# A hybrid attention and MLP step on one core: sixteen-bit transposes by transfer, 33 groups of seven, alternating chunk order in the first part

## The chip, the cores and the metric

The kernel runs on one core of a Trainium2 chip. The metric is the device time of one execution in microseconds. The engines are PE (TensorE: matmuls and transposes), DVE (VectorE), ACT (ScalarE), POOL (GpSimd) and SP (SyncE, which here only issues transfers); sixteen DMA engines carry the transfers that SP, ACT and POOL issue. PEld is the loading of the stationary operand into PE.

## The reference

One layer for 128 context tokens and 128 latent tokens, model width 2048, in float32:

```
sh1, sc1, g1, sh2, sc2, g2 = split(silu(c) @ w_ada + b_ada)
h  = rms_norm(x) * (1 + sc1) + sh1
qa, ka, va, qb, kb, vb, ga, gb = split(h @ w_in)        # 2048 x 8704
oa = windowed attention (qa, ka, va);  ob = neighbourhood attention (qb, kb, vb)
x  = x + g1 * ((sigmoid(ga) * (oa @ w_br_a) + sigmoid(gb) * (ob @ w_br_b)) @ w_out)
h2 = rms_norm(x) * (1 + sc2) + sh2
x  = x + g2 * (relu(h2 @ w_up) ** 2 @ w_down)           # 2048 x 8192 x 2048
```

Both token groups use the same weights, so a weight tile is read once and multiplied with both (the index `s` or `tb`, 0 or 1). The outputs are the two token groups and the keys and values of the context.

## The kernel before

**Products in three parts.** A float32 product is made of three matmuls: each operand is split into a high half (rounded to the matmul's type) and a low half (the rest), and high x high, high x low and low x high are summed in PSUM. For a weight tile `raw` [128, 1024] (two blocks of 128 rows, 512 columns) ACT makes the high half (`copy`, line 86, tile `wH`) and DVE the low half by a subtraction (line 234, tile `wL`). For some steps (`LO_DMA`) the low half is made by ACT and an accumulating transfer of POOL's queue instead (`minus_plus`, line 238). Activations are split in the same way (`split`, line 88).

**Steps.** The program is a list of 456 steps, one for each weight tile of 512 KB, in an order fixed by hand. `run` (line 257) goes through them: it issues the loads of SP up to step i + `LOAD` + `RUN[i]` (4 plus a digit), prepares the halves up to step i + `LOOK[i]` (a digit), emits the step's matmuls (`mm`) and then what the calendar holds for the step (`at(i, fn)`). Every engine works through its own instructions in that order. Tiles of 4 KB per partition come from one ring of 48 buffers (`G`, line 76); a load waits until its buffer is free.

**The parts.** Steps 0 to 71 are the first part: nine units of 512 columns of `w_in` (`first_units`), whose 2048 rows are taken in five chunks (`CHUNKS`, tiles of 128 rows: 2, 2, 2, 4, 6). For each chunk all nine units are run in the same order (`start_steps`, line 370). At the end of a unit's chunk ACT copies the two PSUM accumulators to SBUF (first chunk, `first_evac`) or DVE adds them there (line 393). Meanwhile the modulation is computed (`w_ada` on PE as `ps_ada`, or as dot products on DVE, line 1278, `DOTS1`, `DOTS`, `DOTS2`). Steps 72 to 135 are the gate columns of `w_in` with the attention between them; steps 136 to 167 the branches (`br_unit`, line 805), 168 to 199 `w_out`. Then come the sixteen units of `w_up` (512 columns each), in pairs (`PIECES`), with the `w_down` units of the pair before: the pair p + 1 of `w_up` (16 steps), then the four `w_down` units of pair p (16 steps).

**Groups of seven.** In pairs 1 to 7 of `w_up` a position (two steps) is either plain, 8 products, or one of the positions in `FAST`, where the 2 x 2 block product (two token groups, two blocks of rows, two units) is made of seven products of sums (`up_pair`, line 1058; `prep_y`, line 1115). A product is three matmuls. Such a position needs more sums and halves on DVE and ACT.

**Transposes.** Matmuls contract over partitions, so the merged branches (four tiles) and the sixteen results of `w_up` have to be transposed before they are multiplied on. `tT` (line 792) does this on PE: for each token group four transposes of 128 x 128 into one PSUM bank (`ps_T`, line 797), a copy by ACT (the high half) and a subtraction by DVE (line 800). Its calls stand two steps after a branch unit's end (line 823), in `up_unit` and `up_pair` for the first two `up` tiles, and at `T_PAIR` steps after a pair's end for the others (line 1237).

**Sums of `w_down`.** A unit's accumulators are added to `dsum` by DVE (line 1210) or, for the units in `SUM_DMA`, copied by ACT and added by an accumulating transfer on POOL's queue (line 1214).

**Gates.** The eight gate tiles wait in SBUF until their branch; those in `AWAY` go to memory and come back (`unit_gate`, `gate_back`).

Of the kernel before, what the change touches and what calls it, by code (L numbers as in the profile page):

```python
# [10 lines left out]
F32 = mybir.dt.float32  # L11
F32R = mybir.dt.float32r
BF16 = mybir.dt.bfloat16
AF = mybir.ActivationFunctionType
OP = mybir.AluOpType
AX = mybir.AxisListType

P = 128
# [13 lines left out]
FB_DVE = 6  # L32
FB1 = 14
H_AT = 41
DOTS1 = [6, 8, 15, 20, 28, 30, 31, 38]
CHUNKS = [2, 2, 2, 4, 6]
NFAST = 8
FAST = {1: (0, 1, 5, 6, 7), 2: (0, 3, 4, 6, 7), 3: (0, 2, 4, 5, 7), 4: (0, 2, 3, 5, 7), 5: (0, 1, 2, 4, 5, 7), 6: (0, 2, 4, 6, 7), 7: (0, 1, 2, 4, 5, 7)}
# [7 lines left out]
LOOK = "523112344222344433223333332123333453344534332454455544344533333544324554444555556665556644444333333333332222122213444544555434333333342344333334333323445565533344456656533344434444445455564546555554444443322355444554433333333434334433333333333654654332334455554444555653323314333422222223443233333332223323365455454443222212233432443334434743443332222333423323333333333325434322223333433323333334555543365365433333332222554442122132334343222223332233345544"  # L46
RUN = "454562331000011222223333322222222222222233345555544455434445554445665555555664543433234334444445665543321222222212444444444444442222222232223344444455544544444444443344343334466644455555554543255444343355556866544443566553333323333345552332222222223445332333333333332211122222332233322211233323323332333223333333332343322211333343333322233333444433643333312222334443322333233322222222322333443434455544333120222222232111233456655566567556322325335553333333"
CONST_AT = [60, 65]
XL_DMA = [40]
ADA_AT = [None, 4, 13, 21, 21, 34, 30]  # L50
XS_AT = {1: 13, 2: 18, 3: 29}
POST = {('kvA', 0): [67, 69, 71], ('qA', 0): [70, 73, 75], ('qA', 1): [74, 76, 82], ('kB', 0): [78, 84, 89], ('qB', 0): [82, 84, 93], ('kB', 1): [85, 90, 93], ('qB', 1): [91, 94, 96]}
JOBS = [[78, 79, 81, 83, 94], [82, 83, 87, 90, 94], [88, 89, 91, 93, 98], [93, 93, 95, 98, 102], [96, 97, 100, 105, 112], [102, 103, 107, 112, 120], [105, 107, 111, 118, 120], [112, 114, 117, 120, 122]]
SS_AT = [48, 56, 66, 75, 139, 139]
T_AT = [4, 4]
PREP_IN = [6, 7]
DOTS = [32, 39, 41, 43, 47, 47, 48, 49, 51, 52, 53, 55, 60, 64, 67, 69, 72, 76, 76, 83, 89, 90, 92, 92, 94, 98, 101, 103, 103, 105, 108, 111, 111, 112, 115, 118, 120, 122, 123, 123, 124, 128, 129, 129, 131, 132, 133, 137, 137, 137, 138, 143, 144, 147, 147, 150, 153, 157, 158, 160, 165, 167, 168, 168, 170, 172, 175, 177, 177, 178, 179, 183]
DOTS2 = [232, 233, 235, 237, 240, 242, 262, 265, 269, 270, 272, 289, 297, 299, 302, 306, 307, 326, 327, 332, 334, 335, 358, 361, 364, 365, 368, 370, 393, 394, 397, 401]
STAT_AT = [-1, -1, 10, 12]
# [5 lines left out]
def tile_hybrid_step(ctx: ExitStack, tc: tile.TileContext, a):  # L65
# [16 lines left out]
    def bank(name, pool_=None):  # L82
        return (pool_ or paux).tile([P, 512], F32, name=name, tag="b")
# [278 lines left out]
    nf = len(first_units)  # L362
    units = {}

    def first_evac(u, acc):
        units[u] = G(f"u_{u[0]}{u[1]}").rearrange("p (s n) -> p s n", s=2)
        for tb in range(2):
            copy(units[u][:, tb, :], acc[tb])

    def start_steps(u, k0, nk):  # L370

        box = {}

        def mm(st, kt):
            if kt == 0:
                box["acc"] = [bank("acc", pacc) for _ in range(2)]
            acc = box["acc"]
            wh, wl = st["hl"]
            last = kt + 2 == nk
            for k in range(2):  # L380
                g, kg = divmod(k0 + kt + k, 4)
                for tb in range(2):
                    sh, sl = hH[g][:, kg, tb, :], hL[g][:, kg, tb, :]
                    pe.matmul(acc[tb], sh, wh[:, k, :], start=kt == 0 and k == 0, stop=False)  # L384
                    pe.matmul(acc[tb], sh, wl[:, k, :], start=False, stop=False)  # L385
                    pe.matmul(acc[tb], sl, wh[:, k, :], start=False, stop=last and k == 1)  # L386
            if not last:
                return
            if k0 == 0:
                first_evac(u, acc)  # L390
                return
            for tb in range(2):
                dve.tensor_tensor(units[u][:, tb, :], units[u][:, tb, :], acc[tb], op=OP.add)
# [384 lines left out]

    def sigmoids():
        for u in gates:  # L780
            if u not in direct:
                sigmoid(u)

    sig_at = end_of(("gA", DIRECT[0] - 1)) + 2
# [2 lines left out]


    mH, mL = [None] * 4, [None] * 4
    mt = {}  # L790

    def tT(src, hi, lo):

        for s in range(2):
            ps = bank("ps_T")
            for k in range(4):
                pe.transpose(ps[:, k * P:(k + 1) * P], src[:, s, k * P:(k + 1) * P], ident)  # L797
            psv = ps.rearrange("p (k t) -> p k t", k=4)
            copy(hi[:, :, s, :], psv)
            dve.tensor_tensor(lo[:, :, s, :], psv, hi[:, :, s, :].bitcast(F32), op=OP.subtract)  # L800

    def HL(name):
# [24 lines left out]

    br0 = len(wsteps)
    for n in range(4):
# [131 lines left out]
    split_unit(a["w_out"], 512 * 3, m_stat, evac_out3, ("out", 3), norm2_at(1, 0))  # L961


    aH, aL = {}, {}
    up_r = {}

    def h2_stat(j):
        return lambda kk, tb: (h2H[j][:, kk, tb, :], h2L[j][:, kk, tb, :])

# [15 lines left out]
        sync.dma_start(t, x1d[n])  # L985
        x1[n] = t.rearrange("p (s n) -> p s n", s=2)

    def up_T(n):
        aH[n], aL[n] = HL(f"a{n}")
        tT(up_r.pop(n), aH[n], aL[n])  # L990
# [12 lines left out]

# [54 lines left out]
    def up_pair(p):  # L1058
# [32 lines left out]
        for pos, is_fast in enumerate(kinds):  # L1091
# [50 lines left out]
            def mm_y(st, b=b, j=j, pos=pos, end=end):  # L1142
# [11 lines left out]
                if pos == 0:  # L1154
                    for name, stat, h, l in todo[0:3]:
                        mm(name, stat, h, l, end)
                    if p == 1:
                        up_T(PIECES[0][1])
# [290 lines left out]
```

## Time and profile before

| | |
|---|---|
| Median of three runs | 1346.45 us (1346.03 to 1346.79) |
| The profiled execution | 1346.98 us |
| Its span, first to last instruction | 1344.9 us |
| Granted TensorE clock | 0.997 |
| Bytes moved | 385.44 MB, 287 GB/s |

The profile has a page (busy time of each engine, the span in slices, the DMA queues, the chain of work that ended last, the costliest groups) and views of the same trace: busy time in stretches ("windows"), waits by releaser, the instructions of one tile, the chain in order of time, the timeline. A group's row reads: line, engine, operation, out<-in, form, count, then busy time in us, mean ns of one, and the idle time before it with what ended it. A row of the chain is its start, its length and what it was. A row of windows has each engine's busy time and, in brackets, its count of instructions; PEclk is the granted clock, and the DMA share is the mean busy share of the sixteen DMA engines. Matmuls are pipelined: the duration of one is longer than the distance to the next.

### The profile page before, as it was taken

The numbers are of one execution on the slowest core, as the hardware profiler recorded it, in microseconds if no ns is written. First come the engines' busy times: TensorE is split into PE (matmuls) and PEld (weight loads), VectorE is DVE, ScalarE is ACT, GpSimd is POOL, SyncE is SP. The second block draws the span as 40 slices with busy tenths as digits, with TensorE's granted clock in tenths as the row PEclk, the third lists the DMA queues.
The fourth block names the chain that finished last, engine by engine and source line by source line (L and its number), as shares of the span: only waits on it lengthen the run. The fifth ranks groups of instructions, "written<-read, shape, count | busy, mean of one in ns | idle before, by whom it ended". The sixth has DMA issues, their size and how long they took to land.

```text
span 1344.9 us, 18331 instructions
## 1 busy us (share of the span) xinstructions
PE 1331.6 (99%) x6552; PEld 1081.6 (80%) x6552; DVE 1194.9 (89%) x1568; ACT 738.8 (55%) x966; POOL 66.7 (5%) x76
## 2 busy tenths in 40 slices
PE   8899999999999999999999999999999999999998
PEld 4577788888788878888888888888888888888887
DVE  4689999988898999998789999998999999899675
ACT  5524443566656544345666665565665656556540
POOL 0000001332000000000000000000000000000000
PEclk9899999999999999999999999999999999999999
DMA  9999998977688999798466666888798887769942
GB/s 370 410 409 408 404 366 352 375 215 271 193 282 299 377 397 344 284 332 290 175 232 230 240 219 245 271 264 279 231 317 239 265 285 216 267 191 302 373 151 93
DMA packets 109611, 385.44 MB, mean 287 GB/s; under 512 B 12368, under 2 KB 13584, under 8 KB 109520
## 3 DMA queue, kind: packets, MB, share of 16 engines
q1 hardware_dynamic: 104064, 365.05, 73.5%
q0 software_dynamic: 5312, 19.14, 7.5%
q8 instruction: 51, 0.84, 0.3%
q14 instruction: 40, 0.33, 0.1%
q10 hardware_dynamic: 144, 0.08, 0.0%
HBM read 369.25 MB, written 7.11 MB: 280 GB/s over the span
## 4 chain that ended last, share of the span: by engine, by line
PE 96%; DMA 3%; DVE 1%; issue 0%; ACT 0%; SPq 0%; DVEq 0%
PE acc L284 17%; PE acc L286 17%; PE acc L285 17%; PE Q L1068 6%; PE Q L1070 6%; PE Q L1069 6%; PE acc L384 4%; PE acc L386 4%; PE acc L385 4%; PE ps_ada L301 2%; DMA raw<-in_w_in 2%; PE ps_T L797 1%; PE ps_S L700 1%; DMA araw<-in_w_pair 1%; PE Z L1070 1%; PE Z L1069 1%
## 5 line engine op out<-in xcount | busy, mean ns | idle before, releaser
L234 DVE TENSOR_TENSOR wL<-raw,wH 128x1024 fp32r<-128x1024 f32 x361 | 430.7, 1225 | 79.6 <-ACT wH L86 72.6
L86 ACT ACTIVATE wH<-raw 128x1024 fp32r<-128x1024 f32 (+1 forms) x385 | 385.6, 1047 | 138.6 <-PE acc L285 33.0
L384 PE MATMUL acc<-wH,hH 128*128 128x512 f32 x276 | 109.9, 398 | 0.0
L386 PE MATMUL acc<-wH,hL 128*128 128x512 f32 x276 | 108.4, 393 | 0.7 <-DVE hL L90 0.7
L385 PE MATMUL acc<-wL,hH 128*128 128x512 f32 x276 | 108.5, 393 | 0.0
L284 PE MATMUL acc<-wH,hH 128*128 128x512 f32 x256 | 101.8, 398 | 0.0
L286 PE MATMUL acc<-wH,hL 128*128 128x512 f32 x256 | 99.8, 390 | 0.0
L285 PE MATMUL acc<-wL,hH 128*128 128x512 f32 x256 | 99.7, 389 | 0.0
L1278 DVE CUSTOM_DVE_ANT_0 aT<-aT,cB,cols 128x1024 f32<-128x1024 f32 x56 | 71.5, 1284 | 0.2
L1278 DVE CUSTOM_DVE_ANT_0 junk<-aT,cB,cols 128x1024 bf16<-128x1024 f32 x56 | 71.3, 1279 | 0.0
L86 ACT ACTIVATE tH<-t 128x1024 fp32r<-128x1024 f32 x37 | 39.3, 1062 | 56.9 <-DVE t L1123 42.0
L384 PEld LDWEIGHTS acc<-wH,hH 128*128 128x128 f32 x276 | 52.3, 190 | 14.2 <-issue 3.3
L386 PEld LDWEIGHTS acc<-wH,hL 128*128 128x128 f32 x276 | 52.4, 190 | 12.3 <-DVE hL L90 1.1
L385 PEld LDWEIGHTS acc<-wL,hH 128*128 128x128 f32 x276 | 52.4, 190 | 10.5
L86 ACT ACTIVATE uH<-raw 128x1024 fp32r<-128x1024 f32 x37 | 39.3, 1063 | 36.2 <-DVE raw L1128 35.2
L286 PEld LDWEIGHTS acc<-wH,hL 128*128 128x128 f32 x256 | 48.1, 188 | 10.3
L285 PEld LDWEIGHTS acc<-wL,hH 128*128 128x128 f32 x256 | 48.1, 188 | 9.6 <-issue 0.2
L284 PEld LDWEIGHTS acc<-wH,hH 128*128 128x128 f32 x256 | 48.1, 188 | 9.6 <-issue 0.2
L1123 DVE TENSOR_TENSOR t<-raw 128x1024 f32<-128x1024 f32 x37 | 45.1, 1220 | 5.8 <-PE Z L1069 1.9
L1176 ACT ACTIVATE up<-up 128x1024 f32<-128x1024 f32 x28 | 29.7, 1062 | 33.0 <-DVE up L1170 32.6
L86 ACT ACTIVATE dsum<-acc 128x512 f32<-128x512 f32 x38 | 22.0, 595 | 45.2 <-PE acc L286 42.1
L1133 DVE TENSOR_TENSOR uL<-raw,uH 128x1024 fp32r<-128x1024 f32 x37 | 45.1, 1219 | 0.1
(629 smaller groups left out, 3320.4 us busy)
## 6 DMA issues: line engine op xcount, KB each, us to landing
raw<-in_w_in SPq DMA_DIRECT2D x133, 512.0 KB, 6.7
raw<-in_w_down SPq DMA_DIRECT2D x128, 512.0 KB, 5.9
araw<-in_w_pair SPq DMA_DIRECT2D x80, 512.0 KB, 9.6
raw<-in_w_upF SPq DMA_DIRECT2D x74, 512.0 KB, 5.2
aT<-in_w_gT SPq DMA_DIRECT2D x64, 512.0 KB, 6.6
raw<-in_w_up SPq DMA_DIRECT2D x54, 512.0 KB, 5.1
aT<-in_w_adaT SPq DMA_DIRECT2D x48, 512.0 KB, 7.4
raw<-in_w_out SPq DMA_DIRECT2D x32, 512.0 KB, 9.5
```

The source lines that it names most:

```text
L86: act.activation(out, in_, AF.Copy)
L234: dve.tensor_tensor(st["lo"], st["raw"], st["hi"].bitcast(F32), op=OP.subtract)
L284: pe.matmul(acc[tb], sh, wh[:, k, :], start=f, stop=False)
L285: pe.matmul(acc[tb], sh, wl[:, k, :], start=False, stop=False)
L286: pe.matmul(acc[tb], sl, wh[:, k, :], start=False, stop=l)
L384: pe.matmul(acc[tb], sh, wh[:, k, :], start=kt == 0 and k == 0, stop=False)
L385: pe.matmul(acc[tb], sh, wl[:, k, :], start=False, stop=False)
L386: pe.matmul(acc[tb], sl, wh[:, k, :], start=False, stop=last and k == 1)
L1068: pe.matmul(acc, stat[0], hi, start=f, stop=False)
L1069: pe.matmul(acc, stat[0], lo, start=False, stop=False)
L1070: pe.matmul(acc, stat[1], hi, start=False, stop=l)
L1278: dve.tensor_tensor_reduce(out, box["raw"], cB[s, tag], 1.0, dst if second else baT[:, part, fb:fb + 1], OP.mult, OP.add, dst)
```

## The change

Four things are done together, with the constants of the order set anew.

1. *Transposes by transfer.* For the sixteen `up` tiles and three of the four merged tiles (`M_TE` keeps the last on PE) the calls of `tT` give way to three steps of the calendar. `part`: ACT copies the low and the high 16 bits of each float32 into two planes of a `U16` tile. `flip`: SP issues one transposing transfer of that tile, 16 blocks of 128 x 128, into another tile. `join`: ACT puts the two planes together again into a float32 tile, and `split` makes the two halves (a copy on ACT, a subtraction on DVE). `flip` stands one step (`FLIP`), for the merged tiles two steps, after `part`; `join` stands 3 to 5 steps after `flip` for the tiles of the later pairs, 6 for the merged ones, and 1 and 3 for the first two `up` tiles.
2. *Groups of seven* go from 37 to 33: `FAST[1]` from 5 to 3, `FAST[2]` from 5 to 4, `FAST[5]` from 6 to 5.
3. *First part.* Every second chunk takes the units in reverse, so that the last unit of a chunk is the first of the next; its two accumulators stay in PSUM across the turn.
4. *Placement.* `LO_DMA` goes from 18 to 12 steps, `XL_DMA` from one to none, `SUM_DMA` from 15 to 10 units, `AWAY` from three to six gate tiles, which come back earlier (`GATE_BACK` 3 to 8). `LOOK`, `RUN` and the lists of steps are set anew; their mean over a part changes by less than about one step.

```
 FAST before = {1: (0, 1, 5, 6, 7), 2: (0, 3, 4, 6, 7), 3: (0, 2, 4, 5, 7), 4: (0, 2, 3, 5, 7), 5: (0, 1, 2, 4, 5, 7), 6: (0, 2, 4, 6, 7), 7: (0, 1, 2, 4, 5, 7)}
 FAST after  = {1: (0, 3, 7), 2: (0, 2, 6, 7), 3: (0, 2, 4, 5, 7), 4: (0, 2, 4, 5, 7), 5: (0, 3, 4, 5, 7), 6: (0, 2, 4, 5, 7), 7: (0, 1, 2, 4, 5, 7)}
-SUM_DMA = [5, 6, 9, 10, 11, 12, 13, 15, 16, 19, 20, 21, 23, 25, 27]
+SUM_DMA = [5, 6, 11, 13, 16, 19, 21, 23, 25, 27]
-AWAY = [('gA', 1), ('gB', 0), ('gA', 2)]
+AWAY = [('gA', 1), ('gB', 2), ('gB', 3), ('gA', 0), ('gB', 0), ('gA', 2)]
-GATE_BACK = 3
+GATE_BACK = 8
-LO_DMA = [70, 83, 86, 107, 131, 176, 184, 186, 196, 233, 242, 292, 314, 328, 357, 379, 402, 435]
+LO_DMA = [70, 83, 107, 131, 176, 184, 233, 292, 314, 328, 402, 404]
-XL_DMA = [40]
+XL_DMA = []
-T_PAIR = [[11, 11], [7, 15], [13, 13], [16, 16], [9, 9], [12, 12], [12, 12]]
+T_PAIR = [[8, 9], [6, 8], [8, 9], [7, 8], [10, 11], [8, 9], [12, 11]]
+P_PAIR = [[4, 2], [2, 4], [3, 4], [1, 3], [6, 6], [3, 3], [6, 5]]
+M_TE = (3,)
+M_AT = [1, 3, 9]
+FLIP = 1
+P_UP = [4, 1]
+T_UP = [6, 5]
...
-    def start_steps(u, k0, nk):
+    def start_steps(u, k0, nk, held, hold):
...
-                box["acc"] = [bank("acc", pacc) for _ in range(2)]
+                box["acc"] = open_acc.pop(u) if held else [bank("acc", pacc) for _ in range(2)]
...
-            if k0 == 0:
+            if hold:
+                open_acc[u] = acc
+                return
+            if u not in units:
                 first_evac(u, acc)
                 return
...
-    for nk in CHUNKS:
-        for u in first_units:
-            start_steps(u, k0, nk)
+    for c, nk in enumerate(CHUNKS):
+        for j, u in enumerate(first_units[::-1] if c % 2 else first_units):
+            start_steps(u, k0, nk, c > 0 and j == 0, c < len(CHUNKS) - 1 and j == nf - 1)
...
+    def halves(key, name):
+        return gp.tile([P, 2048], U16, name=f"{name}{key[0]}{key[1]}", tag="g")
+
+    def part(key, src):
+        src = src.rearrange("p s (k f) -> p k s f", k=4).bitcast(U16).rearrange("p k s (f h) -> p h k s f", h=2)
+        planes[key] = halves(key, "pl")
+        dst = planes[key].rearrange("p (h k s f) -> p h k s f", h=2, k=4, s=2)
+        for h in range(2):
+            copy(dst[:, h], src[:, h])
+
+    def flip(key):
+        pl, planes[key] = planes[key], halves(key, "pT")
+        sync.dma_start_transpose(planes[key].rearrange("p (j t) -> p j t", t=P), pl)
+
+    def join(key, hi, lo):
+        full = G(f"fT{key[0]}{key[1]}")
+        copy(full.bitcast(U16).rearrange("p (c h) -> p h c", h=2), planes.pop(key).rearrange("p (h c) -> p h c", h=2))
+        split(hi.rearrange("p k s t -> p (k s t)"), lo.rearrange("p k s t -> p (k s t)"), full)
...
-        at(end_of(("yb", n)) + 2, trans)
+        if n in M_TE:
+            at(end_of(("yb", n)) + 2, trans)
+        else:
+            e = end_of(("yb", n))
+            at(e + M_AT[0], lambda: part(("m", n), mt.pop(n)))
+            at(e + M_AT[1], lambda: flip(("m", n)))
+            at(e + M_AT[2], trans_end)
...
-        if n != PIECES[0][1]:
-            at(end_of(("up", n)) + 2, lambda: up_T(n))
+        at(end_of(("up", n)) + P_UP[n], lambda: up_planes(n))
+        at(end_of(("up", n)) + P_UP[n] + FLIP, lambda: up_flip(n))
+        at(end_of(("up", n)) + T_UP[n], lambda: up_T(n))
...
-            for n, i in zip(PIECES[p + 1], T_PAIR[p]):
-                at(len(wsteps) + i, lambda n=n: up_T(n))
+            for n, i, j in zip(PIECES[p + 1], P_PAIR[p], T_PAIR[p]):
+                at(len(wsteps) + i, lambda n=n: up_planes(n))
+                at(len(wsteps) + i + FLIP, lambda n=n: up_flip(n))
+                at(len(wsteps) + j, lambda n=n: up_T(n))
```

More of the change, by code (lines that the diff above doesn't have):

```diff
@@ L13 @@
 BF16 = mybir.dt.bfloat16
+U16 = mybir.dt.uint16
 AF = mybir.ActivationFunctionType
@@ L34 @@
 H_AT = 41
-DOTS1 = [6, 8, 15, 20, 28, 30, 31, 38]
+DOTS1 = [11, 17, 20, 28, 28, 31, 34, 37]
 CHUNKS = [2, 2, 2, 4, 6]
 NFAST = 8
-FAST = {1: (0, 1, 5, 6, 7), 2: (0, 3, 4, 6, 7), 3: (0, 2, 4, 5, 7), 4: (0, 2, 3, 5, 7), 5: (0, 1, 2, 4, 5, 7), 6: (0, 2, 4, 6, 7), 7: (0, 1, 2, 4, 5, 7)}
-SUM_DMA = [5, 6, 9, 10, 11, 12, 13, 15, 16, 19, 20, 21, 23, 25, 27]
-AWAY = [('gA', 1), ('gB', 0), ('gA', 2)]
-GATE_BACK = 3
+FAST = {1: (0, 3, 7), 2: (0, 2, 6, 7), 3: (0, 2, 4, 5, 7), 4: (0, 2, 4, 5, 7), 5: (0, 3, 4, 5, 7), 6: (0, 2, 4, 5, 7), 7: (0, 1, 2, 4, 5, 7)}
@@ L50 @@
-ADA_AT = [None, 4, 13, 21, 21, 34, 30]
+LOOK = "443323444122344433223333332123333453344534333554455544344534333543324554444555556665556644444333333333332222122312344544555434333333342344333334333323445566643344456656533344434444445455564546555553444554322355444554433333333434334533333333333654544332334455543444555653215536544523333334543233333332223323365455455443222212233432443334434642333334444544534434333333333325434222223333434444444434555642255353443444442222432331122132223342112223332233345544"
@@ new lines @@
+RUN = "301110000000010212223333322222222221111122244455544355434445554334554445555664543433234334444445665543321222222212444444444444442222222232223344444455544544444444555455454445566644455555554543365434343355445756644443566664333312222234552332223333334545332333333333322211122222332233322212233323323332332112344444442343322211333343334323233334544422742222212223445554422333233322222211222333333435767545333110221112232111233456655566567556433435335553333334"
+CONST_AT = [65, 67]
+XL_DMA = []
@@ L61 @@
+DOTS2 = [230, 232, 234, 235, 236, 237, 240, 243, 255, 263, 265, 269, 270, 288, 301, 301, 307, 328, 328, 331, 333, 334, 358, 360, 361, 363, 366, 368, 391, 391, 395, 399]
+STAT_AT = [-1, 0, 10, 16]
+T_PAIR = [[8, 9], [6, 8], [8, 9], [7, 8], [10, 11], [8, 9], [12, 11]]
[5 more added lines that the diff above has]
+T_UP = [6, 5]
 COL = {"qA": 0, "kvA": 1024, "qB": 1536, "kB": 2560, "vB": 3584, "gA": 4608, "gB": 6656}
@@ L363, in tile_hybrid_step @@
     units = {}
+    open_acc = {}
     def first_evac(u, acc):
@@ L383, in mm @@
                     sh, sl = hH[g][:, kg, tb, :], hL[g][:, kg, tb, :]
-                    pe.matmul(acc[tb], sh, wh[:, k, :], start=kt == 0 and k == 0, stop=False)
+                    pe.matmul(acc[tb], sh, wh[:, k, :], start=kt == 0 and k == 0 and not held, stop=False)
                     pe.matmul(acc[tb], sh, wl[:, k, :], start=False, stop=False)
-                    pe.matmul(acc[tb], sl, wh[:, k, :], start=False, stop=last and k == 1)
+                    pe.matmul(acc[tb], sl, wh[:, k, :], start=False, stop=last and k == 1 and not hold)
             if not last:
                 return
-            if k0 == 0:
+            if hold:
+                open_acc[u] = acc
+                return
+            if u not in units:
                 first_evac(u, acc)
@@ L780, in sigmoids @@
         for u in gates:
-            if u not in direct:
+            if u not in direct and u not in AWAY:
                 sigmoid(u)
@@ L789, in tile_hybrid_step @@
     mH, mL = [None] * 4, [None] * 4
+    aH, aL = {}, {}
+    up_r = {}
     mt = {}
@@ L800, in tT, with up_planes, up_flip, up_T @@
             dve.tensor_tensor(lo[:, :, s, :], psv, hi[:, :, s, :].bitcast(F32), op=OP.subtract)
+    planes = {}
+    def halves(key, name):
[13 more added lines that the diff above has]
+        split(hi.rearrange("p k s t -> p (k s t)"), lo.rearrange("p k s t -> p (k s t)"), full)
+    def up_planes(n):
+        part(("a", n), up_r.pop(n))
+    def up_flip(n):
+        flip(("a", n))
+    def up_T(n):
+        aH[n], aL[n] = HL(f"a{n}")
+        join(("a", n), aH[n], aL[n])
     def HL(name):
@@ L825, in trans, with trans_end @@
             tT(mt.pop(n), mH[n], mL[n])
-        at(end_of(("yb", n)) + 2, trans)
+        def trans_end():
+            mH[n], mL[n] = HL(f"m{n}")
+            join(("m", n), mH[n], mL[n])
+        if n in M_TE:
[5 more added lines that the diff above has]
+            at(e + M_AT[2], trans_end)
     br0 = len(wsteps)
@@ L961, in tile_hybrid_step @@
     split_unit(a["w_out"], 512 * 3, m_stat, evac_out3, ("out", 3), norm2_at(1, 0))
-    aH, aL = {}, {}
-    up_r = {}
     def h2_stat(j):
```

19 lines of the change are left out of this document (5 added, 14 removed).

## The prediction

> **What bounds the kernel now.** I read the page first, then PE's own waits, the chain of waits, and the busy time by stage.
>
> ```profile
> span 1344.9 us, 18331 instructions
> PE 1331.6 (99%) x6552; PEld 1081.6 (80%) x6552; DVE 1194.9 (89%) x1568; ACT 738.8 (55%) x966; POOL 66.7 (5%) x76
> PE 96%; DMA 3%; DVE 1%; issue 0%; ACT 0%; SPq 0%; DVEq 0%
> PE ps_ada L301 <- DMA araw<-in_w_pair: 4.2, 8, 0.7
> ```
>
> The chain that ended last is PE for 96% of the span, and PE's longest wait by releaser adds up to 4.2 us. So PE runs without holes; the time is a startup and then the sum of what PE is given. DVE follows at 89%. An edit counts if it changes PE's list, or makes PE wait where it waits for nothing now.
>
> The stages: first part (44 to 257 us), gates and attention (to 478), branches (to 570), `w_out` and the first two `w_up` units (to 702), the pairs of `w_up` units with `w_down` (to 1287), the last `w_down` units.
>
> ```profile
> core 0: us, PE busy (x) PEld busy (x) DVE busy (x) ACT busy (x) POOL busy (x), PEclk, DMA share, GB/s
> 44.00:257.00 213.00, 212.28 (x1248) 166.20 (x1245) 199.07 (x300) 92.61 (x113) 14.28 (x12) 0.99 0.99 387
> 478.00:570.00 92.00, 92.00 (x473) 75.19 (x473) 90.50 (x125) 39.02 (x45) 0.00 (x0) 1.00 0.90 335
> 570.00:702.00 132.00, 132.00 (x607) 109.79 (x606) 111.50 (x154) 78.65 (x112) 5.05 (x8) 1.00 0.75 260
> 702.00:1287.00 585.00, 585.00 (x2634) 485.36 (x2633) 540.49 (x627) 355.88 (x403) 20.77 (x24) 1.00 0.79 260
> ```
>
> PE fills every stage at a granted clock of 0.99 to 1.00. What is left of others: in the branches DVE has 1.5 us free and the DMA engines 10% of 92 us, 9.2 us; in the stage of the pairs DVE has 44.5 us free and the DMA engines 21% of 585 us, 122.9 us.
>
> **PE: transposes removed.** Each tile [128, 1024] costs eight transposes on PE.
>
> ```profile
> L797 PE MATMUL ps_T<-ident,up x128: 270/272/273, 681.4 to 1288.2; 128*128 128x128 f32 x128
> L797 PE MATMUL ps_T<-ident,g_gA x32: 270/273/276, 500.2 to 568.9; 128*128 128x128 f32 x32
> 523.00 0.88 PE ps_T L797 x8
> 545.66 0.87 PE ps_T L797 x8
> 681.58 0.87 PE ps_T L797 x8
> 1286.73 1.75 PE ps_T L797 x16
> ```
>
> A transpose lasts 272 ns, but they overlap: eight hold the chain for 0.87 us, sixteen for 1.75. The change takes away all 128 of the `up` tiles (sixteen tiles) and 24 of the 32 of the merged tiles (three; the fourth stays on PE by `M_TE`): 19 x 0.87 = 16.6 us off PE.
>
> **PE: products added.** Groups of seven go from 37 to 33 (`FAST[1]` loses two, `FAST[2]` and `FAST[5]` one each). A group is two steps with 7 products of 3 matmuls, 21; two plain steps have 24. The price of a matmul follows from the chain rows above: 523.00 to 545.66 is one branch unit of 8 steps of 12 matmuls and one block of transposes, so (22.66 - 0.88) / 96 = 0.227 us. 4 x 3 x 0.227 = 2.7 us more on PE.
>
> Nothing else of PE's list changes. Sum: -16.6 + 2.7 = -13.9 us.
>
> **First part.** Chunks go forwards and backwards in turn, so the unit that ends one chunk begins the next and keeps its two banks. Eight additions from PSUM (four turns, two banks) go away:
>
> ```profile
> L393 DVE TENSOR_TENSOR u_qA<-u_qA,acc 128x512 f32<-128x512 f32 x16 | 10.3, 680 | 0.0
> ```
>
> 8 x 0.680 = 5.4 us off DVE. This stage has 212.28 us of PE work in 213 and the DMA engines at 0.99: 0 us of the end. The other edits of constants here (loads of the modulation, dots moved by a few steps) move work under the same cover; if it failed, DVE (199.07 of 213) would be late first.
>
> **DVE, ACT and transfers, beside PE.**
>
> ```profile
> L234 DVE TENSOR_TENSOR wL<-raw,wH 128x1024 fp32r<-128x1024 f32 x361 | 430.7, 1225 | 79.6 <-ACT wH L86 72.6 <-issue 2.6 <-PE ps_PT L746 2.6
> L1123 DVE TENSOR_TENSOR t<-raw 128x1024 f32<-128x1024 f32 x37 | 45.1, 1220 | 5.8 <-PE Z L1069 1.9 <-PE Q L1069 1.7 <-DMA raw<-in_w_upF 1.2
> L1126 DVE TENSOR_TENSOR raw<-t,raw 128x512 f32<-128x512 f32 x37 | 25.6, 692 | 1.3
> L1210 DVE TENSOR_TENSOR dsum<-dsum,acc x18: 677/683/689, 842.9 to 1284.0; 128x512 f32<-128x512 f32 x18
> L86 ACT ACTIVATE XH<-raw 128x1024 fp32r<-128x1024 f32 x37 | 38.9, 1051 | 4.0 <-PE Q L1069 2.4 <-DMA raw<-in_w_upF 1.3 <-PE Q L1070 0.3
> L86 ACT ACTIVATE dsum<-acc x38: 573/598/601, 750.1 to 1296.7; 128x512 f32<-128x512 f32 x38
> ```
>
> A group of seven has on DVE four operations like 1.22 and three like 0.69, 6.95 us; two plain steps have 2 x 1.225 = 2.45. Four fewer: -18.0. Coming to DVE: six low halves out of `LO_DMA` and one out of `XL_DMA`, 7 x 1.22 = 8.5; five sums out of `SUM_DMA`, 10 x 0.683 = 6.8. A join subtracts 1.22 at once where two from PSUM took 2 x 0.68: -0.14 each, -2.7. With the first part's 5.4: DVE -10.8, to 1184 of 1331 us, 89% as before. It stays beside PE.
>
> ACT pays for the transfers: two copies of 1024 halves, one of 2048, and one copy in the split. By the 1.05 us of 1024 elements that is 5 x 1.05 = 5.25 against 2 x 0.60 from PSUM: +4.05 x 19 = 77 us, 56.7 of them (14) in the stage of the pairs: 413 of 576. No row shows a copy of 16-bit elements with strides; 5.25 is taken, half of the two strided parts the lower bound (2.1 saved each) and double the upper one (4.2 more each): even that leaves ACT at 82% there. Hidden behind PE.
>
> Transfers removed: 12 from POOL (seven low halves, five sums). Added: three more gate tiles to memory and back (six of 512 KB), and 19 transposes on SP.
>
> ```profile
> q1 hardware_dynamic: 104064, 365.05, 73.5%
> q0 software_dynamic: 5312, 19.14, 7.5%
> DMA to landing us min/median/max: 4.8/7.7/9.1
> 847.94 0.80 SPq L208 DMA_DIRECT2D raw<-in_w_upF  x2
> SPq L208 <- PE acc L286: 257.6, 80, 9.3
> ```
>
> On POOL's queue 7.5% of 1344.9 us is 100.9 us of all sixteen engines for 19.14 MB: 2.76 us for 512 KB. On SP's it is 988.5 us for 365.05 MB, 1.42 us. So 12 x 2.76 = 33 us go and 6 x 1.42 = 8.5 come.
>
> **The unknown: a transpose by transfer.** No row shows one. Lower bound: an ordinary transfer, 1.42 us of the engines. Upper bound: the transfer moves pieces of one row of a 128x128 block, 256 bytes, 2048 of them, each at the price of a packet of SP's queue (73.5% of 16 x 1344.9 us / 104064 = 0.152 us): 2048 x 0.152 / 16 = 19.5 us. The nearest row is the transfer from SBUF to SBUF, `dsum` (its landing is the 4.8/7.7/9.1 above): I take 2.8 us of the engines and 8 us to landing. Then 14 x 2.8 = 39 us stand against 122.9 free plus 28 freed (ten of the twelve) in the pairs, and 2 x 2.8 against 33 in the stage before. In the branches three transposes and one more gate tile read back make 9.8 us against 9.2 free, at the edge; the loads run some steps ahead there, so I cost it at 0.
>
> The Trainium skill has two prices. "VectorE: DVE Perf Modes", section "The three transpose paths", gives 1309 ns for a 128x128 block of bf16 on the DMA path. "DMA: Bandwidth & Descriptors", section "Latency and other measured facts", gives a transpose 261 GB/s with a non-contiguous middle dimension. An estimate from these pages is 16 x 1.309 = 20.9 us if a tile's blocks go one after another, or 2.0 us at the rate; the sum by the second is the forecast, by the first the rival of the late transposes. No run here shows either.
>
> The wait it adds: SP holds the transfer until ACT's two plane copies are done, and behind it stand the weight loads in SP's order, seven or so steps ahead of use (`LOAD` 4 and `RUN`). ACT's join waits for the landing, and behind it on ACT stand the next copies `wH`, then DVE's low halves, then PE. A step is 12 x 0.227 = 2.7 us. In the pairs the join is placed 3 to 5 steps after the transfer (8.2 to 13.6 us), so 8 us to landing cost nothing; if it is later, the copies of `wH` are late next, covered by `LOOK`'s two to five steps. Only the first `up` tile has one step: up to 8 - 2.7 = 5.3 us once on ACT, inside that cover. Of the issue itself SP's 0.40 us (two in 0.80) is the lower bound; SP already waits 257.6 us for PE to free buffers, so several us more delay nothing by themselves.
>
> Sum against the profiled execution: 1344.9 of span lies in 1346.98 us, 0.5 above the median 1346.45. 1346.98 - 13.9 = 1333.1, or 1332.6 by the median. PE's waits leave a few us either way; I forecast 1333.
>
> **The rivals.** All start from -13.9.
>
> *Some is given back*, chance 0.12. In the branches DVE (90.50 of 92, then about 90.1 of 89.4) and the DMA engines are both full; in the pairs the joins push ACT. 3 to 10 us lost: about 1339. For it: those two numbers. Against: PE waits nowhere there today, and the lookahead can fetch work earlier.
>
> *The same*, 0.05: about 14 us are given back, 1346. At 7.2 us of the engines per transpose the branches alone do this (3 x 7.2 + 1.4 - 9.2 = 13.8).
>
> *Late transposes: slower*, 0.19. Place: DMA engines in the branches, then in the pairs, with ACT's join and SP's loads behind. It decides from 7.2 us per transpose; at 10.8 us (where 14 of them use up 122.9 + 28 in the pairs) the branches lose 3 x 10.8 + 1.4 - 9.2 = 24.6, so 1333 + 24.6 = 1357; at the bound of 19.5 it is 51 in the branches, 6 before the pairs (39 - 33) and 122 in them (273 - 151): about 1512. For it: DMA shares of 0.79 and 0.90, and 256-byte pieces. Against: the sum of bytes is small, 19 x 0.52 = 10 MB beside the 384 of both queues.
>
> *The change does not remove PE's transposes* has no chance worth a number: the calls stand in the diff.
>
> **How the numbers follow.** Forecast 0.64, its own range 1329 to 1337 (PE's few us of waits below; above, half of the join waits). The median can tell 0.2%, 2.7 us, from no change, which is 1343.8 to 1349.1. Faster: 0.64 + 0.12 = 0.76; same 0.05; slower 0.19. The range reaches from 1329 down to the start of the slower rival, about 8.3 us per transpose (3 x 8.3 + 1.4 - 9.2 = 17 over 1333): 1350. The bound of 19.5 stays outside, in the part left out.
>
> **What would show it.** Right: PE's rows at the transposing line fall from 160 to 8, PE has no new wait over 1 us in total per line, the 512-column matmuls grow by 12, DVE is near 1184 us and ACT near 800, the transposing transfers land in under 10 us, and the stage of the pairs is 9 to 10 us shorter. Wrong: PE or its weight loads waiting for `wH` or `wL` while ACT waits for a transposed plane; weight loads landing later than today behind a transposing transfer; the branches longer than 92 us.

## The result and the profile after

| | before | after |
|---|---|---|
| Median | 1346.24 us (4 runs, 1344.17 to 1346.79) | 1333.09 us (4 runs, 1332.30 to 1334.14) |
| Span of the profiled execution | 1344.9 us | 1331.4 us |

The ratio is 0.9906 with a 95% interval of 0.9888 to 0.9923: the changed kernel is about 13 us faster, where 13.4 were forecast. The total hides two errors of about 5.5 us with opposite signs, which the rest of this document takes apart. Runs are compared by their medians; a trace shows the one profiled execution.

The page of the changed kernel, in the lines that answer to those of before:

```profile
span 1331.4 us, 18029 instructions
PE 1316.4 (99%) x6411; PEld 1067.2 (80%) x6412; DVE 1185.6 (89%) x1538; ACT 801.2 (60%) x979; POOL 54.0 (4%) x64
DMA packets 148266, 392.24 MB, mean 295 GB/s; under 512 B 51792, under 2 KB 53008, under 8 KB 148176
q1 hardware_dynamic: 144448, 378.16, 78.9%
q0 software_dynamic: 3584, 12.85, 5.0%
PE 93%; DMA 4%; ACT 1%; DVE 1%; issue 0%; SPq 0%; DVEq 0%; ACTq 0%
```

PE still bounds the kernel. DVE is at 1185.6 us (forecast 1184) and ACT at 801.2 (forecast near 800). Its stages, in the same stretches as before:

```profile
44.00:257.00 213.00, 212.75 (x1237) 167.52 (x1235) 200.12 (x301) 92.90 (x114) 14.86 (x16) 1.00 0.99 386
478.00:570.00 92.00, 92.00 (x414) 76.17 (x413) 90.46 (x120) 59.14 (x58) 0.86 (x1) 1.00 1.03 363
...
702.00:1287.00 585.00, 581.32 (x2553) 479.44 (x2552) 536.86 (x611) 405.38 (x416) 13.93 (x16) 1.00 0.82 266
```

Other than before, PE is not full in the stage of the pairs: 3.7 us are empty. PE's own waits name it:

```profile
PE Q L1123 <- ACT dsum L93: 3.6, 1, 3.6
PE ps_ada L308 <- DMA araw<-in_w_pair: 2.7, 5, 0.6
```

PE's transposing line has eight rows left, those of the merged tile that stays on PE:

```profile
L812 PE MATMUL ps_T<-ident,g_gA x8: 270/272/273, 559.7 to 560.5; 128*128 128x128 f32 x8
```

The transposing transfers, by the tile they write (`pTa`, the `up` tiles; duration of the issue on SP as minimum, median and maximum in ns), their time to landing, and the copies into the planes:

```profile
L834 SPq DMA_TRANSPOSE pTa<-pla x16: 1777/3102/8063, 676.6 to 1258.5; - x16
DMA to landing us min/median/max: 4.2/5.5/11.0
```

```profile
L93 ACT ACTIVATE pla<-up x32: 1039/1042/1060, 674.6 to 1253.1; 128x1024 uint16<-128x1024 uint16 x32
```

Both kernels give PE the same list apart from the transposes and the 12 extra matmuls, so the start of each part can be set side by side. From the starts of PE's matmuls in the two traces, us:

```
part begins        before     after     ahead by
branches           468.54    462.79       5.75
w_out              562.71    554.27       8.44
pair 1             698.63    689.31       9.32
pair 7            1211.50   1194.35      17.15
w_down, pair 6    1251.21   1239.31      11.90
w_down, pair 7    1296.49   1282.83      13.66
end               1344.9    1331.4       13.5
```

Two lines were not forecast: 5.75 us are there before the first transpose is due, and 5.25 are lost within pair 7. Between these, each stretch moves by its transposes (0.9 a tile) and by the matmuls of the four lost groups. With the matmuls counted at 0.2268 us, the excess of each unit over its matmuls falls by 16.6 us in total where transposes stood, and the four groups add 12 x 0.2268 = 2.7. So: -5.75 - 16.6 + 2.7 + 5.3 (pair 7) + 0.9 (small waits in pairs 3 to 5 and at the end) = -13.5.

The early gain can be seen on the chain. Before, then after:

```profile
33.68 10.13 DMA araw<-in_w_pair
43.85 1.08 PE ps_ada L301 x8
44.93 0.73 PE acc L384
45.66 0.43 PE acc L385
...
54.14 1.20 DVE junk L1278
...
59.33 0.62 DVE hL L90
...
59.99 0.49 PE acc L386
...
73.43 3.59 PE ps_ada L301 x64
```

```profile
31.18 10.15 DMA araw<-in_w_pair
41.38 0.64 PE ps_ada L308 x8
...
67.22 3.59 PE ps_ada L308 x64
```

The first modulation pair of the step list ends 2.5 us earlier, and the next 6.2 us. SP's queue shows one reason. Before:

```profile
22.10 1.00 SPq L1256 DMA_DIRECT2D cB<-in_crow  x2
23.44 0.33 SPq L208 DMA_DIRECT2D raw<-in_w_in  x1
24.09 9.92 SPq L293 DMA_DIRECT2D araw<-in_w_pair  x8
```

The two broadcast rows `cB`, which only the dot products need, go out ahead of the eight `araw` tiles that PE waits for; in the changed kernel the eight come first, because the dots start at step 11 instead of 6. A second reason is DVE's list: the dot products (`junk` on the chain above) stand ahead of `hL`, and PE waits 0.7 us for it, a wait that the changed kernel does not have:

```profile
PE acc L386 <- DVE hL L90: 0.7, 1, 0.7
```

A third is the granted TensorE clock (PEclk, the third number from the end), first before, then after:

```profile
43.00:50.00 7.00, 6.49 (x27) 4.20 (x21) 2.36 (x2) 3.08 (x4) 0.00 (x0) 0.51 1.03 408
43.00:50.00 7.00, 7.00 (x34) 5.80 (x33) 5.69 (x10) 6.88 (x11) 0.00 (x0) 1.00 1.03 411
```

At 0.51 the matmuls on the chain of before start 0.43 us apart, where 0.23 is the distance at 1.0: twelve of them take 5.25 us (44.93 to 50.18) in place of 2.7. So of the 6.2 us about 2.5 are the earlier loads, about 3 the clock, and the rest is the wait for `hL`. Why the clock fell in one of the two executions and not in the other is not shown.

The late loss begins with one wait. ACT's timeline shows what stands ahead of the copy that PE waits for:

```profile
1195.81 1.06 ACT L93 ACTIVATE tH<-t 128x1024 fp32r<-128x1024 f32 x1 [2.02 <-DVE t L1178]
1197.87 1.06 ACT L93 ACTIVATE uH<-raw 128x1024 fp32r<-128x1024 f32 x1 [1.00 <-DVE raw L1183]
1198.83 1.07 ACT L93 ACTIVATE dsum<-acc 128x512 f32<-128x512 f32 x2
```

The copy of `dsum` would free two PSUM banks for the next pair. It stands behind the preparation of that pair's second group of seven (`tH`, `uH`), and this waits for DVE. DVE had stood idle twice for the joins just before, and has no idle time from 1184.4 us to the copy:

```profile
1179.63 1.23 DVE L97 TENSOR_TENSOR a12L<-fTa,a12H 128x1024 fp32r<-128x1024 f32 x1 [1.81 <-ACT a12H L93]
1183.29 1.22 DVE L97 TENSOR_TENSOR a13L<-fTa,a13H 128x1024 fp32r<-128x1024 f32 x1 [2.44 <-ACT a13H L93]
```

The wait is 3.6 us of the 5.3. Behind it the granted clock is 0.5 for 3.4 us, in which PE does half of its work, and that is the other 1.7:

```profile
1201.00:1204.00 3.00, 3.00 (x9) 2.32 (x8) 2.93 (x5) 1.42 (x2) 0.06 (x1) 0.50 0.99 199
```

### The profile page after: what moved, and what is told of

Its sections match the earlier page's. It is cut to its first block, busy times and chain, and to the rows that moved or that the text cites. A ratio compares the mean times of both kernels' runs of the same rounds, so it can differ in the third digit from the quotient of the medians.

```text
span 1331.4 us, 18029 instructions
## 1 busy us (share of the span) xinstructions
PE 1316.4 (99%) x6411; PEld 1067.2 (80%) x6412; DVE 1185.6 (89%) x1538; ACT 801.2 (60%) x979; POOL 54.0 (4%) x64
## 4 chain that ended last, share of the span: by engine, by line
PE 93%; DMA 4%; ACT 1%; DVE 1%; issue 0%; SPq 0%; DVEq 0%; ACTq 0%
PE acc L291 17%; PE acc L292 17%; PE acc L293 17%; PE Q L1123 6%; PE Q L1124 6%; PE Q L1125 6%; PE acc L394 4%; PE acc L395 4%; PE acc L396 4%; DMA araw<-in_w_pair 3%; PE ps_ada L308 2%; PE ps_S L713 1%; PE Z L1124 1%; PE Z L1123 1%; PE Z L1125 1%; DMA aT<-in_w_adaT 1%
## 5 line engine op out<-in xcount | busy, mean ns | idle before, releaser
L241 DVE TENSOR_TENSOR wL<-raw,wH 128x1024 fp32r<-128x1024 f32 x375 | 446.6, 1224 | 72.2 <-ACT wH L93 67.9
L93 ACT ACTIVATE wH<-raw 128x1024 fp32r<-128x1024 f32 (+1 forms) x393 | 393.0, 1044 | 128.2 <-PE acc L395 22.5
L93 ACT ACTIVATE tH<-t 128x1024 fp32r<-128x1024 f32 x33 | 35.0, 1061 | 57.7 <-DVE t L1178 55.0
L394 PEld LDWEIGHTS acc<-wH,hH 128*128 128x128 f32 x276 | 51.8, 188 | 13.5 <-issue 2.9
L293 PEld LDWEIGHTS acc<-wH,hL 128*128 128x128 f32 x256 | 48.1, 188 | 10.2
L93 ACT ACTIVATE uH<-raw 128x1024 fp32r<-128x1024 f32 x33 | 35.1, 1062 | 32.0 <-DVE raw L1183 27.7
L308 PE MATMUL ps_ada<-araw,cpad 128*32 128x256 f32 x640 | 39.1, 382 | 2.9 <-DMA araw<-in_w_pair 2.7
L93 ACT ACTIVATE fTa<-pTa 128x2048 uint16<-128x2048 uint16 x16 | 40.5, 2534 | 2.0 <-PE acc L292 1.4
L1178 DVE TENSOR_TENSOR t<-raw 128x1024 f32<-128x1024 f32 x33 | 40.2, 1220 | 1.0 <-PE acc L292 1.0
## 6 DMA issues: line engine op xcount, KB each, us to landing
araw<-in_w_pair SPq DMA_DIRECT2D x80, 512.0 KB, 10.2
```

The source lines that it names most:

```text
L93: act.activation(out, in_, AF.Copy)
L241: dve.tensor_tensor(st["lo"], st["raw"], st["hi"].bitcast(F32), op=OP.subtract)
L293: pe.matmul(acc[tb], sl, wh[:, k, :], start=False, stop=l)
```

## The experiments

**The early dots alone.** The kernel before, with one constant of the change.

```
-DOTS1 = [6, 8, 15, 20, 28, 30, 31, 38]
+DOTS1 = [11, 17, 20, 28, 28, 31, 34, 37]
```

> The kernel before with one constant of the change: the eight early dot products of the modulation (DOTS1) start at step 11 where they started at step 6. Theory (the change's 5.8 us in the first part come from these dots: their loads no longer stand in SP's order ahead of the first modulation pair, and their 10 us on DVE no longer stand ahead of the first splits of h): branches begin 5 to 6 us earlier, time about 1340.6. Rival (the gain comes from the turning order and the kept accumulators, which take eight additions off DVE): first part as before, 1346 within 1 us.

Measured: 1345.30 us, ratio 1.0001 (0.9992 to 1.0010). The trace shows both halves of it: by the 140th 512-column matmul the kernel is 6.44 us ahead of before, by the 400th 6.06, by the 600th only 1.52. Between these PE waits three times for `araw` and `S`, about 0.6 us each, and once for `wL`; the wait for `wL` is new, and the one for `S` comes twice where it came once:

```profile
PE acc L385 <- DVE wL L234: 1.6, 1, 1.6
...
PE ps_sel L319 <- ACT S L86: 1.1, 2, 0.6
```

So the dots' new places come with the early gain, and alone they do not keep it. Part of the gain is the clock, which is at 1.0 in this trace from 43 to 50 us. The expectation was half right: it named the place and missed that the work moved later would be paid there. At the same granted clock the edit gains nothing at all: the six executions with a clock of 1.0 took 1345.03 to 1345.48 us, and the four of the kernel before beside them 1343.86 to 1344.52.

**The turn alone.** The order of the units and the kept accumulators, put into the kernel before.

```
+    for c, nk in enumerate(CHUNKS):
+        for j, u in enumerate(first_units[::-1] if c % 2 else first_units):
+            start_steps(u, k0, nk, c > 0 and j == 0, c < len(CHUNKS) - 1 and j == nf - 1)
```

> The kernel before with the turning order of units and the kept accumulators alone. Theory (PE had no wait there that the eight additions of 0.68 us caused): 1346 within 1 us, DVE 5.4 us less busy. Rival (the turn makes the first part's gain): about 1340.5.

Measured: 1344.08 us, ratio 0.9995 (0.9985 to 1.0004). It is 1.1 us ahead from the 100th matmul on, and 1.4 at the last. DVE is 4.2 us less busy (1190.7 for 1194.9), where 5.4 were expected. The rival falls; the theory was right within what the runs can tell, though 1344.08 is a little under its range.

**Both together, and then with the modulation's places.** First the two edits above, then also the changed kernel's `ADA_AT` and `SS_AT`.

```
-ADA_AT = [None, 4, 13, 21, 21, 34, 30]
+ADA_AT = [None, 4, 13, 18, 21, 36, 29]
-SS_AT = [48, 56, 66, 75, 139, 139]
+SS_AT = [43, 51, 73, 75, 139, 139]
```

> The kernel before with the later early dots and the turning order together. The dots alone gained 6.4 us by the 140th product and gave 4.9 back between 140 and 190 us. Theory (what gives it back is DVE being full there, and the 5.4 us that the turn takes off DVE pay for it): the branches begin 5 to 6 us earlier than before, time about 1340.5. Rival (the two gains only add, 1.5 and 1.1 us): about 1343.5.

> The kernel before with the later early dots, the turning order and, new, the changed kernel's places of the modulation pairs (ADA_AT and SS_AT). Dots and turn together were 4.85 us ahead at the 400th product and 2.7 at the end of the first part; the changed kernel keeps 5.3. Theory (the rest is lost where a modulation pair stands too late for the dots' new places, and these two lists give it back): branches begin 5.3 to 5.8 us earlier than before, time about 1340.5. Rival (RUN, LOOK or the later dots do it): 2.7 us earlier as without the lists, about 1343.5.

Measured: 1344.00 us (0.9989, 0.9980 to 0.9997) and 1345.17 us (0.9992, 0.9983 to 1.0000). Both expectations failed by their time, 1340.5: in each the rival's 1343.5 is nearer. Dots and turn are 4.85 us ahead at the 400th matmul and keep 2.67. (Their trace has 3.4 us at a clock of 0.5 near 43 us, so some 1.7 of the difference to the dots alone is the clock.) With the places, 5.83 are kept up to the 800th, the whole head start of the changed kernel, as the theory had it; but 4.2 of them go at the first gate unit, where PE's transposition waits for DVE to finish `kvA`:

```profile
PE ps_qT L658 <- DVE u_kvA L635: 1.7, 1, 1.7
PE ps_qT L658 <- DVE u_kvA L645: 0.9, 1, 0.9
```

The waits are 2.6 us; the rest is the clock, which is low just behind them:

```profile
253.00:257.00 4.00, 3.08 (x11) 2.40 (x10) 3.32 (x6) 0.00 (x0) 1.02 (x2) 0.57 1.03 410
```

The changed kernel places that transposition four steps later (`POST`, step 75 for 71), which fits, but that edit was not tried alone. Shown is that dots, turn and places together keep the early gain to the end of the first part, that the dots alone and dots with turn do not, and that neither the dots nor the turn alone moves the time by more than its interval. The places without the turn were not tried.

**All transposes back on PE.** The changed kernel, with `tT` at the steps where the planes were made.

```
-M_TE = (3,)
+M_TE = (0, 1, 2, 3)
     def up_planes(n):
-        part(("a", n), up_r.pop(n))
+        aH[n], aL[n] = HL(f"a{n}")
+        tT(up_r.pop(n), aH[n], aL[n])
```

> The changed kernel with all twenty tiles transposed on PE again, at the step at which the changed kernel makes the planes; everything else as changed. Theory (19 tiles cost PE 0.87 us each, and the one stall of 5.3 us before the pair of units 14 and 15 comes from ACT's joins): 16.6 us back and the stall gone, 1333.1 + 16.6 - 5.3 = 1344. Rival (the joins cost PE nothing, the stall has another cause): 1349.5. If the transposes hardly counted: 1333 to 1338.

Measured: 1345.40 us, ratio 0.9997 (0.9989 to 1.0006), 12.3 us over the changed kernel. In its trace the excess over the matmuls is 1.76 us in each `w_down` stretch that has transposes again, and pair 7 has 0.24 in place of 5.50. The theory holds nearly in its time, 1344: the transposes cost PE their time (nineteen tiles at 0.88), and the late wait belongs to the transposing by transfer. That it belongs to ACT's joins within it, as the theory had it, this run cannot tell; the two on the join below speak against their place.

**The group count.** The changed kernel with the 37 groups of before (`FAST`).

> The changed kernel with the 37 groups of seven of before. Theory (PE's 12 matmuls fewer are worth 2.7 us only if DVE can follow; four groups cost it 18 us, 9 of them in pair 1, and its free time in the stage of the pairs falls from some 45 to 27 us): PE gets new waits for halves or sums in pairs 1, 2 or 5, so 1331 to 1340, not better than 1331. Rival (33 is no better than 37, DVE has room): 1330.4 with no new wait.

Measured: 1347.48 us, ratio to before 1.0016 (1.0007 to 1.0025): slower than the kernel before, and 14.4 us over the changed one. PE's waits:

```profile
PE acc L291 <- ACT up L93: 3.0, 1, 3.0
...
PE acc L291 <- DVE up L1223: 2.3, 3, 1.5
PE Q L1124 <- DVE XL L1186: 1.7, 2, 1.5
PE Q L1124 <- DVE uL L1188: 1.6, 2, 1.0
```

By stretch, pair 1 and the `w_down` units after it have 8.1 us over their matmuls (0.0 in the changed kernel), pair 2 and the units after it 1.9, pair 5 and the units after it 4.8: just where groups were put back. The expected waits came, and the loss was over the range expected. Part of it is the clock again: the trace has 10.2 us at 0.5, the last few us left out, where the changed kernel has 3.4. `LOOK`, `RUN` and the calendar stayed as set for 33 groups; 37 with settings of their own were not tried.

**The late wait: the join.** The changed kernel, the join of unit 13 five steps later.

```
-T_PAIR = [[8, 9], [6, 8], [8, 9], [7, 8], [10, 11], [8, 9], [12, 11]]
+T_PAIR = [[8, 9], [6, 8], [8, 9], [7, 8], [10, 11], [8, 14], [12, 11]]
```

> The changed kernel with one number changed: the join of unit 13 stands 14 steps after the end of its pair, where it stood 9. Theory (two joins of 3.6 us on ACT in a row push the copy of dsum that frees the PSUM banks behind a preparation that waits for DVE, and PE waits 4 us): the wait goes, pair 7 is 5 us shorter, about 1328. Rival (DVE is simply full in that stretch, the lateness comes back a few steps on): 1333 within 1 us.

Measured: 1332.89 us (0.9907, 0.9891 to 0.9923), as the changed kernel. Pair 7 has 5.79 us over its matmuls, and the wait is the same:

```profile
PE Q L1123 <- ACT dsum L93: 3.9, 1, 3.9
```

The theory falls: that the two joins stand in a row is not what holds the copy. The rival's time came.

**The late wait: the order on ACT.** The changed kernel with two digits of `LOOK`, so that fewer preparations stand ahead of that copy.

```
-LOOK[406], LOOK[407] = 5, 3
+LOOK[406], LOOK[407] = 3, 2
```

> The changed kernel with two digits of LOOK changed, at the last two steps before pair 7, so that the copy of dsum of that w_down unit stands on ACT ahead of the preparation of the pair's second group. Theory (PE's one long wait is for the two banks that this copy frees, and the copy is held up only by the order on ACT): the 5.3 us in pair 7 go, about 1328. Rival (DVE is behind there, PE waits for the halves of the second group in place of the bank): 1331 to 1333.5.

Measured: 1330.96 us (0.9892, 0.9879 to 0.9906). The wait for `dsum` is gone from the list, and a smaller one for DVE has taken its place:

```profile
PE Q L1124 <- DVE XL L1186: 1.7, 2, 1.5
```

Pair 7 keeps 2.66 us over its matmuls and the units after it get 0.8; the clock stays at 1.0. The time is at the lower edge of the rival's. Both readings were half right: the order on ACT made the wait longer, and under it DVE is behind.

> The changed kernel with the two digits of LOOK and the join of unit 13 five steps later. With the digits alone pair 7 kept 2.7 us over its matmuls, PE waiting 1.7 us for DVE's low half XL. Theory (DVE stood idle 1.8 and 2.4 us for the two joins just before and has no room to make it up in a pair with six groups): 1 to 3 us less than with the digits alone, 1328 to 1330. Rival (the loads of that pair come late behind the two transposing transfers, whatever the joins do): 1331 within 1 us.

With the later join on top of the two digits: 1330.88 us (0.9888, 0.9873 to 0.9903), pair 7 at 2.62. The place of the join is not it in this form either: DVE begins the pair's first group 3.5 us earlier (1183.84 for 1187.38) and its second only 1.0, held by the moved join for 1.30 us. The rival's time came, but not its reason as far as the trace shows: of late loads there is one wait, 1.5 us of ACT.

**Fewer groups in pair 7.** The two digits, and pair 7 with five groups of seven.

```
-7: (0, 1, 2, 4, 5, 7)
+7: (0, 2, 4, 5, 7)
```

> The changed kernel with the two digits of LOOK and pair 7 with five groups of seven in place of six. Theory (DVE is the limit in pair 7: six groups are 6 x 6.95 + 2 x 2.45 = 46.6 us on DVE for 39.5 on PE): PE's list grows by 0.7 us, the 2.7 and 0.8 us of waits in pair 7 and behind it go, about 1328. Rival (the wait has its cause before pair 7 and stays): 1331.7.

Measured: 1328.81 us (4 runs, 1327.58 to 1328.90), ratio to before 0.9871 (0.9858 to 0.9884). PE's empty time in the stage of the pairs falls from 3.7 us to 1.0, and the theory's time came:

```profile
702.00:1287.00 585.00, 584.00 (x2574) 482.02 (x2573) 536.35 (x611) 407.55 (x419) 13.93 (x16) 1.00 0.82 266
```

Pair 7 has no excess over its matmuls, so here the 0.7 us of PE that the sixth group saves cost more in waiting. By the count six groups are 46.6 us of DVE for 39.5 of PE. The count alone does not decide: five are 42.1 for 40.1 and do not wait, and six did not wait in the kernel before (0.24 us over) nor with all transposes on PE. So it must matter how far ahead DVE is when the pair begins, which is argued and not shown; what sets it back with the transposes by transfer stays open. This kernel is better than both.

**Twice the transfers.** The changed kernel, where each transposing transfer is followed by a second one into a tile that nobody reads; then by a plain copy of the same planes instead.

```
         sync.dma_start_transpose(planes[key].rearrange("p (j t) -> p j t", t=P), pl)
+        sync.dma_start_transpose(halves(key, "again").rearrange("p (j t) -> p j t", t=P), pl)
...
+        sync.dma_start(halves(key, "again"), pl)
```

> The changed kernel with every transposing transfer issued twice, the second into a tile that nobody reads. One took 3.2 us of all sixteen DMA engines and held SP 3.1 us (median) in the changed kernel. Theory (transfers have room: 19 x 3.2 = 61 us more against the idle share): 1333 to 1336. Rival (the branches, whose DMA share is full, and the stretch before pair 7, where SP was held 9.4 us by two of them, pay for it): 1338 to 1350.

> The changed kernel with a plain transfer of the same 512 KB from the same planes into a tile that nobody reads, behind every transposing transfer, on SP. Twice the transposing transfer cost 24.5 us. Theory (that cost was the transposing transfer itself, 3.2 us of the engines and some 3 us of SP each): the plain one costs half or less, 1335 to 1342. Rival (it was the one more buffer of the ring, or the wait of SP for the planes, which the plain copy has too): 1352 to 1360.

Measured: 1357.55 us (1.0095, 1.0079 to 1.0112) with the second transposing transfer, 24.5 us over the changed kernel; 1342.91 us (0.9978, 0.9969 to 0.9986) with the plain copy, 9.8 over it. The two have the same extra buffer and the same wait for the planes; the rows of the second transfers differ in the time that SP is held (first the transposing, then the plain one):

```profile
L835 SPq DMA_TRANSPOSE againa<-pla x16: 1848/2640/5213, 682.2 to 1287.9; - x16
```

```profile
L835 SPq DMA_DIRECT2D againa<-pla x16: 487/563/1257, 679.4 to 1274.3; - x16
```

For the second transposing transfer the theory (1333 to 1336) and its rival (1338 to 1350) were both too small. For the plain copy the theory of half the cost or less holds, with 1342.9 just over its range, and its rival falls. Of the 24.5 us, 9.8 go with the buffer, the longer-held planes and 512 KB of plain bytes, and the other 14.7 with the transposing transfer itself. Some of each is the clock: at 0.5 it stood, the last few us left out, for 17.1 us with the transposing transfer, 6.8 with the plain copy and 3.4 in the changed kernel, about half of which PE loses. Which of the transfer's two prices does the rest (SP held 2.6 us, or the DMA engines) is open. In the first run the losses lie in the first three `w_out` units (3.7 us), in the `w_down` units of pair 1 (6.4), in pair 6 and the units of pair 5 (7.1) and in pair 7 (4.0 more); the branches lose nothing.

## Why the prediction was right, and where it was not

*PE's transposes, -16.6 us: right.* Its signs came: eight transposes are left and the 512-column matmuls are 12 more. The excess over the matmuls falls by 16.6 us, and putting the transposes back costs 12.3, near to 16.6 less the late wait of 5.3.

*PE's products, +2.7 us: right as a term, and wrong in how the step saw it.* The prediction counted the lost groups as a cost. Put back under the same settings, 37 groups leave nothing of the gain (1347.5 us): where they were put back, PE waits for DVE and ACT.

*The first part, 0 us: wrong.* The step that failed is the sentence that the other edits of constants there "move work under the same cover". PE was 212.28 us busy in 213 and was taken to be full, but a matmul at a clock of 0.5 counts as busy for its longer time, and the late start of the modulation pair lies in part ahead of 44 us: before the 140th matmul some 6 us were to be had. About 2.5 were the dots' rows ahead of `araw` in SP's queue, about 3 the clock of 0.51 from 43 to 50 us, and the rest a wait for `hL` behind the dots on DVE. The clock is in no term of the prediction, and part of the 5.75 is luck: which execution was profiled. The eight additions, which the prediction named, are worth 1.1 us alone.

*The work beside PE hidden, 0 us: wrong in one place.* ACT's part was costed at 5.25 us a tile and measured 2 x 1.04 + 2.53 + 1.06 = 5.67, so 85 us for 77. All of it is hidden but before pair 7, where 5.3 us came out: a wait of 3.6 and the low clock behind it. So two signs failed, no new wait over 1 us and a stage of the pairs that is 9 to 10 us shorter: from the start of pair 1 to the last `w_down` units it is 4.3 us shorter. The step that failed is the one that took the stage's free time on DVE and ACT as a whole: 44.5 us free in 585 says nothing about a pair with six groups. The runs show that the wait goes with the transposes by transfer (all on PE: 0.24), with the order on ACT (5.5 to 2.7) and with the sixth group (0.0); what makes DVE late stays open.

*The transfer: right value, wrong reading of the bounds.* It was taken at 2.8 us of the sixteen engines and 8 us to landing; the trace has 3.2 (the 256-byte packets added up, over 19) and 5.5, with a longest landing of 11.0 where under 10 was the sign; the join stands 3 to 6 steps after it, not 3 to 5 (6 for the second tile of pair 1). The pieces are as counted, 38912 packets of 256 bytes, 2048 a tile; but such a packet takes 18 ns (median) where 4 KB take 159, so the upper bound of 19.5 us, which gave each the price of a full packet, was far off. The Trainium skill's rate ("DMA: Bandwidth & Descriptors", "Latency and other measured facts"), 2.0 us by estimate, is nearer to the 3.2 than its 1309 ns a block one after another ("VectorE: DVE Perf Modes", "The three transpose paths"), 20.9 us by estimate.

*The rival of the late transposes: its point was set too high and its place was wrong.* It was to decide from 7.2 us a tile and to strike first in the branches. Two transfers of about 3 us a tile gave 1357.6, and the branches lost nothing although their DMA share is 1.05 in that run: that share had no say there. It struck `w_out`, the pairs and their `w_down` units instead. The sentence that several us more on SP "delay nothing by themselves" was not shown either: the doubled transfers speak against it, though they do not part SP from the DMA engines.

*The sum came out at 1333 because 5.75 us gained and 5.3 lost nearly cancel.* The mechanism of the main term is shown; the closeness of the total is chance.

## What to carry to other kernels

Where PE is full, a transpose moved to a transfer was worth PE's time for it (0.88 us a tile here), but the engines beside PE must then do the same work in less time: count what they have to give up as part of the change. Take the room of an engine by the tightest stretch, not by the stage. And look at the order of instructions on the engine that frees a buffer: a copy that PE waits for may stand behind work that could have come after it. Compare the granted clock of two traces in the same stretch before an edit gets the credit for a difference.

## What the hardware showed that was not expected

A transposing transfer of 512 KB held SP for 3.1 us (median, up to 8.1), where a plain one is issued in 0.40 (two in 0.80). Its 2048 pieces of 256 bytes cost the engines about twice a plain transfer (3.2 against 1.42 us), not fourteen times. ACT copied 1024 16-bit elements with a stride, into the planes, in 1.04 us, as fast as float32, but took 2.53 us for the 2048 of the join, where 2 x 1.05 was assumed. A DMA share of 1.03 over 92 us in the branches went with no loss on PE at all. And a wait of PE of 3.6 us cost 5.3: the granted clock was 0.5 for 3.4 us behind it, in the changed kernel and in the one with the later join (a wait of 3.9), while it stayed at 1.0 behind the shorter waits of the kernel with the two digits (1.7 us in two). These runs do not show what decides it.
